# Expert numbers found in two 16-rank steps over all heads, and one-hot rows for spreading made by other engines

## The chip, the core and the metric

The kernel runs on one core of one Trainium2 chip. A core has five engines that run side by side: TensorE (PE in the profile, its weight loads PEld) multiplies matrices, VectorE (DVE), ScalarE (ACT) and GpSimd (POOL) work element by element, and SyncE (SP) starts transfers. Each engine takes its instructions in the order in which they stand in its own queue; semaphores tie the queues together. The metric is the device time of one execution in microseconds (us), lower is better.

## What is computed

One layer of a flow-matching backbone is applied to two streams, a prompt of 256 tokens (P) and a sample of 1024 tokens (Q). After a token mixer comes a layer of 16384 single-neuron experts with product keys. The change lies in that layer alone:

```python
q = (xb @ w_query).reshape(PEER_TOKEN_BLOCK, PEER_HEADS, 2, PEER_HALF)
s = jnp.einsum("thpk,pnk->thpn", q, sub_keys).astype(jnp.float32)
top_s, top_i = lax.top_k(s, PEER_TOPK)
cand_s = top_s[:, :, 0, :, None] + top_s[:, :, 1, None, :]
cand_i = top_i[:, :, 0, :, None] * N_KEYS + top_i[:, :, 1, None, :]
...
best_s, best_j = lax.top_k(cand_s, PEER_TOPK)
idx = jnp.take_along_axis(cand_i, best_j, axis=-1)
g = jax.nn.softmax(best_s, axis=-1)
u = u_tab[idx]
act = jax.nn.gelu(jnp.einsum("td,thkd->thk", xb, u).astype(jnp.float32))
v = v_tab[idx]
return jnp.einsum("thk,thkd->td", (g * act).astype(xb.dtype), v)
```

There are 8 heads, 128 keys on each side, 16 best of each side, and 16 best of their pairs. A token thus has 128 expert numbers (first key times 128 plus second key) and 128 gates.

## The kernel before

Tokens are handled in blocks of 128, one token a partition: two blocks of P, eight of Q. `route` (line 906) chooses the experts of a block. It finds the 16 best of each side by VectorE's eight-at-a-time maximum (lines 917 to 921), adds scores and expert numbers for the 50 pairs that can be among the best 16 (lines 925 to 933, tiles `cs` and `ci`), and finds the 16 best pairs of each head, `bv`, with their places `pu` among the 50 (lines 938 to 942). Then, head by head, it turns places into expert numbers: VectorE compares the 16 places with 50 numbers (`hot`, line 948, 800 elements), GpSimd multiplies by the expert numbers (`oh`, line 950), VectorE sums over the 50 (line 951). Last come the gates `g`, by ScalarE's exponential.

Two ways lead on from there. Blocks of P and the last three of Q go to `experts`: GpSimd gathers the rows of both expert tables one expert at a time for all 128 tokens (tile `row`, line 1010), and VectorE multiplies and adds them (lines 1023 and 1032). These rows run as a long background of the whole kernel. `PACE` ties the gathers of Q to marks that `spread` sets, three gathers to a mark. The first five blocks of Q (`DB`) are computed densely instead: TensorE multiplies all experts, and the gates have to stand in a table of 128 x 128 experts for every token. `spread` (line 1038) makes that table. For four tokens a step, 32 steps a block, it makes one-hot rows of the first key times the gate (`oa`) and of the second key (`ob`), multiplies them on TensorE (line 1068), and ScalarE copies the product into the block's table `G` (line 1069). When 32 steps are done, SyncE stores `G` to memory in eight transfers (line 1071, tile `d_GD`). `G` has one buffer, in the pool `stage`, so the next block fills it only after that store has read it. The one-hots come from one VectorE compare of both keys in bfloat16 (`hot`, line 1058); ScalarE widens the second key's to `ob` (line 1059), and the first key's are multiplied by the gate on GpSimd in one step (line 1061) and on ScalarE, four times a step, in the next (line 1065).

The stage that does this (lines 1257 to 1267) handles the blocks in the order 0, 1, 5, 2, 3, 4, 6, 7, routes each, spreads those below five, and beside that computes the dense first layer of 56 of 128 table tiles (`first_layer`, TensorE's products `bank<-hTh,uh` and the like, with `ul` split off on GpSimd). After it, `dense` does the rest. The order of the instructions on each engine is made by a scheduler that plays the program through when it is built; the code's order is only its starting point, so one edit can move instructions elsewhere.

## Time and profile before

| what | value |
|---|---|
| time, median of 3 runs | 5130.33 us (5128.91 to 5131.31) |
| the profiled execution | 5135.52 us, span 5133.7 us |
| TensorE busy | 4395.7 us, 86% |
| VectorE busy | 4081.8 us, 80% |
| GpSimd busy | 3155.0 us, 61% |
| ScalarE busy | 2023.5 us, 39% |
| TensorE's granted clock, mean | 0.925 of full speed |

The profiled execution is one run of the program with every instruction recorded; its span goes from the first to the last recorded instruction. A busy share over the whole span mixes stages with different limits, so the rows further down are cut to the stretch of 2640 to 3616 us in which blocks are routed and spread. In a row of groups stand the line of the code, engine, operation, output tile <- input tiles, shapes, count, then busy time in us and mean of one in ns, then the idle time of the engine just before and what ended it. In a row of one line or tile stand the shortest, the median and the longest duration in ns, and when the first and the last one started.

### The profile page before, as it was taken

The page shows a single profiled execution, that of the slowest core. Times are in us where ns is not written, and L with a number is a line of the kernel's source. Part 1 is how long each engine was busy: PE and PEld are TensorE (multiplying, and loading weights), DVE is VectorE, ACT ScalarE, POOL GpSimd, SP SyncE. Part 2 cuts the span into 40 slices and gives each one's busy share as a digit, 9 for nine tenths or more (in the row PEclk, how much of TensorE's full clock was granted, in tenths as well). Part 3 has the DMA queues.
Part 4 walks back from the last instruction along what each step waited for, and adds up shares of the span by engine and source line. Part 5 has one row for each costly group of instructions (what it writes and reads, how often), then busy time and mean ns, then how long its engine had stood idle before and what let it go on. Part 6 is the DMA issues. An engine that isn't in the chain of part 4 may idle for free.

```text
span 5133.7 us, 68153 instructions
## 1 busy us (share of the span) xinstructions
PE 4395.7 (86%) x23707; PEld 3804.8 (74%) x23707; DVE 4081.8 (80%) x6816; ACT 2023.5 (39%) x3126; POOL 3155.0 (61%) x2290
## 2 busy tenths in 40 slices
PE   6888788899999779799698887874688999999998
PEld 4676677677777678677587877773566799989997
DVE  7778564999995886566769998895688899888997
ACT  4546333336663112212434766776222222222222
POOL 1456451578886765468665576774556677667764
PEclk8999899999999889899899998995899999999999
DMA  6676646698988953478684478877988999899994
GB/s 212 218 242 196 199 144 234 214 322 293 313 305 320 312 174 99 167 290 327 231 289 153 135 238 267 290 264 245 342 314 322 333 337 340 303 343 337 337 339 155
DMA packets 608774, 1346.80 MB, mean 262 GB/s; under 512 B 63743, under 2 KB 283592, under 8 KB 607917
## 3 DMA queue, kind: packets, MB, share of 16 engines
q0 software_dynamic: 187776, 680.61, 37.7%
q1 hardware_dynamic: 412588, 648.20, 37.6%
q10 hardware_dynamic: 8064, 13.64, 0.7%
q8 instruction: 186, 3.05, 0.2%
q14 instruction: 160, 1.30, 0.1%
HBM read 1177.56 MB, written 164.68 MB: 261 GB/s over the span
## 4 chain that ended last, share of the span: by engine, by line
PE 25%; DVE 15%; DMA 6%; issue 5%; POOL 4%; ACT 3%; SPq 2%; ACTq 0%; POOLq 0%; DVEq 0%
PE bank L150 21%; PE bank L159 3%; DVE row L1023 2%; DVE hot L1058 2%; SPq L1071 2%; POOL row L1010 2%; DVE fi L951 1%; DVE y L1032 1%; DMA row<-in_peer_u,idxQ 1%; ACT G L1069 1%; DMA row<-in_peer_v,idxP 1%; POOL vl L193 1%; ACT oa L1065 1%; ACT ob L1059 1%; DVE gt L1118 1%
## 5 line engine op out<-in xcount | busy, mean ns | idle before, releaser
L1032 DVE SCALAR_TENSOR_TENSOR y<-row,act,y 128x1024 f32<-128x1024 f32 x635 | 814.5, 1283 | 146.4 <-DMA row<-in_peer_v,idxP 111.2
L1023 DVE SCALAR_TENSOR_TENSOR row<-row,h 128x1024 f32<-128x1024 f32 x640 | 762.0, 1210 | 129.2 <-DMA row<-in_peer_u,idxP 60.8
L150 PE MATMUL bank<-hTh,ul 128*128 128x320 f32 x2048 | 641.2, 315 | 16.8 <-POOL ul L193 16.7
L150 PE MATMUL bank<-hTh,uh 128*128 128x320 f32 x2048 | 643.2, 314 | 3.7 <-ACT sc L883 3.6
L150 PE MATMUL bank<-hTl,uh 128*128 128x320 f32 x2048 | 641.9, 314 | 0.0
L150 PE MATMUL bank<-vl,wh 128*128 128x512 f32 x1280 | 513.1, 401 | 50.8 <-POOL vl L193 47.4
L1010 POOL DMA_INDIRECT row<-in_peer_v,idxQ x384 | 409.8, 1067 | 230.9 <-DVE y L1032 176.3
L1010 POOL DMA_INDIRECT row<-in_peer_u,idxQ x384 | 404.9, 1054 | 230.2 <-DVE row L1023 136.3
L150 PE MATMUL bank<-vh,wh 128*128 128x512 f32 x1280 | 473.8, 397 | 76.5 <-ACT vh L192 68.5
L193 POOL TENSOR_TENSOR wl<-wr,wh 128x1024 fp32r<-128x1024 f32 x148 | 362.6, 2451 | 273.7 <-ACT wh L192 252.8
L150 PE MATMUL bank<-vh,wl 128*128 128x512 f32 x1280 | 509.3, 398 | 5.1 <-DVE wl L193 4.9
L150 PEld LDWEIGHTS bank<-hTh,ul 128*128 128x128 f32 x2048 | 390.6, 191 | 20.6 <-POOL ul L193 20.4
L150 PEld LDWEIGHTS bank<-hTh,uh 128*128 128x128 f32 x2048 | 392.0, 191 | 5.7 <-ACT sc L883 3.9
L150 PEld LDWEIGHTS bank<-hTl,uh 128*128 128x128 f32 x2048 | 392.0, 191 | 1.4
L192 ACT ACTIVATE wh<-wr 128x1024 fp32r<-128x1024 f32 x176 | 185.7, 1057 | 463.7 <-PE bank L150 187.6
L1068 PE MATMUL bank<-ob,oa 128*128 128x128 f32 x1280 | 225.6, 327 | 152.2 <-ACT G L1069 74.8
L1010 POOL DMA_INDIRECT row<-in_peer_u,idxP x256 | 272.8, 1065 | 132.3 <-DVE row L1023 73.8
L150 PEld LDWEIGHTS bank<-vh,wh 128*128 128x128 f32 x1280 | 243.8, 191 | 132.7 <-ACT vh L192 72.8
L1010 POOL DMA_INDIRECT row<-in_peer_v,idxP x256 | 277.4, 1083 | 93.7 <-issue 30.6
L150 PEld LDWEIGHTS bank<-vl,wh 128*128 128x128 f32 x1280 | 246.9, 193 | 114.1 <-POOL vl L193 56.5
L1068 PEld LDWEIGHTS bank<-ob,oa 128*128 128x128 f32 x1280 | 196.0, 226 | 179.4 <-ACT G L1069 74.7
L150 PEld LDWEIGHTS bank<-vh,wl 128*128 128x128 f32 x1280 | 246.8, 193 | 59.8 <-DVE wl L193 8.0
(442 smaller groups left out, 12457.6 us busy)
## 6 DMA issues: line engine op xcount, KB each, us to landing
raw<-in_peer_uT SPq DMA_DIRECT2D x128, 512.0 KB
raw<-in_peer_v SPq DMA_DIRECT2D x128, 512.0 KB
wr<-in_w_in SPq DMA_DIRECT2D x112, 512.0 KB
d_GD<-G SPq DMA_DIRECT2D x40, 1024.0 KB
gt<-d_GD SPq DMA_DIRECT2D x128, 320.0 KB
w<-in_w_ada SPq DMA_DIRECT2D x48, 512.0 KB
wr<-in_w_query SPq DMA_DIRECT2D x48, 512.0 KB
d_AD<-a SPq DMA_DIRECT2D x56, 320.0 KB
```

Source lines behind the costliest of these rows:

```text
L150: nc.tensor.matmul(out, l, r, start=(i == 0), stop=(i == len(ops) - 1))
L159: nc.tensor.matmul(out, a, b, start=(i + j == 0), stop=(i == KT - 1 and j == len(ops) - 1))
L192: nc.scalar.activation(hi, src, AF.Copy)
L193: note(eng, eng.tensor_tensor(lo, src, hi.bitcast(F32), op=ALU.subtract))
L951: nc.vector.tensor_reduce(idf[:, h, :], oh[:].rearrange("p c k -> p k c"), axis=AX.X, op=ALU.add)
L1010: i = nc.gpsimd.indirect_dma_start(out=t[:], out_offset=None, in_=A[tab], in_offset=bass.IndirectOffsetOnAxis(ap=idx[:, k:k + 1], axis=0))
L1023: nc.vector.scalar_tensor_tensor(t[:], t[:], 1.0, h[:], op0=ALU.mult, op1=ALU.mult, accum_out=act[:, k:k + 1])
L1032: nc.vector.scalar_tensor_tensor(y[:], t[:], act[:, k:k + 1], y[:], op0=ALU.mult, op1=ALU.add)
L1058: nc.vector.tensor_tensor(hot[:].rearrange("p k t q -> p k (t q)"), keys8[:], key[:, None, t0:t0 + 4, :].rearrange("p o t q -> p o (t q)") ...
L1059: nc.scalar.activation(ob[:], hot[:, :, :, 1].rearrange("p k t -> p t k"), AF.Copy)
L1068: nc.tensor.matmul(ps[:, i * P:(i + 1) * P], oa[:, i, :], ob[:, i, :], start=True, stop=True)
L1071: nc.sync.dma_start(GD[j:j + 16, :, b * P:(b + 1) * P].rearrange("j i t -> i j t"), G[:, j:j + 16, :])
```

## The change

Route: the expert number is no longer summed over 50 places. The pairs stand in rows by the rank of the first key, so a place tells the rank: `FIRSTS` lists at which of the 50 places each rank of 16 begins. For all eight heads at once, 16 chosen slots against 16 ranks (2048 elements in bfloat16), VectorE asks which ranks begin at or before the place, sums the differences of the first keys over those ranks (the sum is the first key itself), takes the largest such beginning and subtracts it (the remainder is the second key's rank), compares that with the 16 ranks and sums the second keys. Each sum or maximum over 16 ranks is a fold by halves: 1024, 512, 256 and 128 elements. GpSimd has no part in it. The two keys stay apart in `ij`; blocks that are spread use them so, and shifting and masking in `spread` goes.

Spread: `ob` is now made by VectorE directly, one compare of float32 numbers with four tokens' second keys (512 elements). `oa` is made by GpSimd in every step, one instruction a token that compares 128 numbers with the token's first key and multiplies by its gate. ScalarE makes neither. `oa` and `ob` have three buffers each instead of two.

```diff
 NCAND = 50
+FIRSTS = [sum(n for _, n in PAIRS[:a]) for a in range(9)] + [43 + a for a in range(7)]
 NEG = -3.0e38
...
-    def numbers(pool, n, w):
-        t = pool.tile([P, n, w], BF, name=f"numbers{n}")
-        nc.vector.tensor_copy(t[:], iota_k[:, 0:n, None].to_broadcast([P, n, w]))
-        return t
+    NS = NH * TOPK
+    def rank_tables(pool):
+        ranks = pool.tile([P, TOPK, NH], BF, name="ranks")
+        nc.vector.tensor_copy(ranks[:], iota_k[:, 0:TOPK, None].to_broadcast([P, TOPK, NH]))
+        firsts = pool.tile([P, TOPK, NH], BF, name="firsts")
+        for a in range(TOPK):
+            nc.vector.memset(firsts[:, a, :], float(FIRSTS[a]))
+        return ranks, firsts
...
             nc.vector.max_index(iu[:, g, 8:16], v[:, g, 8:16], S2[:])
-        fi = peer.tile([P, NH, 2, TOPK], F32, tag="fi", name="fi")
-        nc.vector.tensor_copy(fi[:].rearrange("p h q k -> p (h q) k"), iu[:])
-        nc.vector.tensor_scalar(fi[:, :, 0, :], fi[:, :, 0, :], float(NK), None, op0=ALU.mult)
+        keys = peer.tile([P, 2, TOPK, NH], BF, tag="keys", name="keys")
+        nc.vector.tensor_copy(keys[:], iu[:].rearrange("p (h q) a -> p q a h", q=2))
+        steps = peer.tile([P, TOPK, NH], BF, tag="steps", name="steps")
+        nc.vector.tensor_copy(steps[:, 0, :], keys[:, 0, 0, :])
+        nc.vector.tensor_tensor(steps[:, 1:, :], keys[:, 0, 1:, :], keys[:, 0, 0:TOPK - 1, :], op=ALU.subtract)
         vv = v[:].rearrange("p (h q) k -> p h q k", q=2)
         cs = peer.tile([P, NH, NCAND], F32, tag="cs", name="cs")
-        ci = peer.tile([P, NH, NCAND], F32, tag="ci", name="ci")
-        for dst, src in ((cs, vv), (ci, fi[:])):
-            o = 0
-            for a, n in PAIRS:
-                nc.vector.tensor_tensor(dst[:, :, o:o + n], src[:, :, 1, 0:n], src[:, :, 0, a:a + 1].to_broadcast([P, NH, n]), op=ALU.add)
-                o += n
-            nc.vector.tensor_tensor(dst[:, :, o:o + 8], src[:, :, 0, 8:16], src[:, :, 1, 0:1].to_broadcast([P, NH, 8]), op=ALU.add)
+        o = 0
+        for a, n in PAIRS:
+            nc.vector.tensor_tensor(cs[:, :, o:o + n], vv[:, :, 1, 0:n], vv[:, :, 0, a:a + 1].to_broadcast([P, NH, n]), op=ALU.add)
+            o += n
+        nc.vector.tensor_tensor(cs[:, :, o:o + 8], vv[:, :, 0, 8:16], vv[:, :, 1, 0:1].to_broadcast([P, NH, 8]), op=ALU.add)
         bv = peer.tile([P, NH, TOPK], F32, tag="bv", name="bv")
...
             nc.vector.max_index(pu[:, h, 8:16], bv[:, h, 8:16], c2[:])
-        pf = peer.tile([P, NH, TOPK], BF, tag="pf", name="pf")
-        nc.vector.tensor_copy(pf[:], pu[:])
-        idf = fi[:, :, 0, :]
-        for h in range(NH):
-            hot = peer.tile([P, NCAND, TOPK], BF, tag="hot", name="hot", bufs=1)
-            nc.vector.tensor_tensor(hot[:], places[:], pf[:, h, None, :].to_broadcast([P, NCAND, TOPK]), op=ALU.is_equal)
-            oh = peer.tile([P, NCAND, TOPK], F32, tag="oh", name="oh", bufs=1 if s is SQ else 2)
-            nc.gpsimd.tensor_tensor(oh[:], hot[:], ci[:, h, :, None].to_broadcast([P, NCAND, TOPK]), op=ALU.mult)
-            nc.vector.tensor_reduce(idf[:, h, :], oh[:].rearrange("p c k -> p k c"), axis=AX.X, op=ALU.add)
+        place = peer.tile([P, TOPK, NH], BF, tag="place", name="place")
+        nc.vector.tensor_copy(place[:], pu[:].rearrange("p h k -> p k h"))
+        wide = [P, TOPK, TOPK, NH]
+        flat = lambda t: t[:].rearrange("p a k h -> p a (k h)")
+        mask = peer.tile(wide, BF, tag="mask", name="mask")
+        terms = peer.tile(wide, BF, tag="terms", name="terms")
+        half = peer.tile([P, TOPK // 2, NS], BF, tag="half", name="half")
+        def folded(x, op, dst):
+            x, y, n = flat(x), half[:], TOPK // 2
+            while n:
+                nc.vector.tensor_tensor(dst if n == 1 else y[:, 0:n, :], x[:, 0:2 * n:2, :], x[:, 1:2 * n:2, :], op=op)
+                x, y, n = y, x, n // 2
+        def combine(out, of_rank, of_slot, op):
+            nc.vector.tensor_tensor(out[:], of_rank[:, :, None, :].to_broadcast(wide), of_slot, op=op)
+        slots = lambda t: t[:, None].to_broadcast(wide)
         dense = s is SQ and b < DB
...
         tail = "" if dense else f"{s.name}{b}"
-        idx = keep.tile([P, NH * TOPK], I32, name="idx" + tail)
-        nc.vector.tensor_copy(idx[:].rearrange("p (h k) -> p h k", h=NH), idf)
-        g = keep.tile([P, NH, TOPK], F32, name="gw" + tail)
-        nc.vector.tensor_tensor(g[:], bv[:], bv[:, :, 0:1].to_broadcast([P, NH, TOPK]), op=ALU.subtract)
-        nc.scalar.activation(g[:], g[:], AF.Exp)
+        ij = peer.tile([P, 2, 1, NS], F32, tag="ij", name="ij")
+        base = peer.tile([P, TOPK, NH], BF, tag="base", name="base")
+        combine(mask, firsts, slots(place[:]), ALU.is_le)
+        combine(terms, steps, mask[:], ALU.mult)
+        folded(terms, ALU.add, ij[:, 0])
+        combine(mask, firsts, mask[:], ALU.mult)
+        folded(mask, ALU.max, base[:].rearrange("p (o k) h -> p o (k h)", o=1))
+        nc.vector.tensor_tensor(base[:], place[:], base[:], op=ALU.subtract)
+        combine(terms, ranks, slots(base[:]), ALU.is_equal)
+        combine(terms, keys[:, 1], terms[:], ALU.mult)
+        folded(terms, ALU.add, ij[:, 1])
+        if dense:
+            where = ij[:, :, 0, :]
+        else:
+            where = keep.tile([P, NS], I32, name="idx" + tail)
+            nc.vector.scalar_tensor_tensor(ij[:, 0, 0, :], ij[:, 0, 0, :], float(NK), ij[:, 1, 0, :], op0=ALU.mult, op1=ALU.add)
+            nc.vector.tensor_copy(where[:], ij[:, 0, 0, :])
+        e = peer.tile([P, NH, TOPK], F32, tag="e", name="e")
+        nc.vector.tensor_tensor(e[:], bv[:], bv[:, :, 0:1].to_broadcast([P, NH, TOPK]), op=ALU.subtract)
+        nc.scalar.activation(e[:], e[:], AF.Exp)
         sm = peer.tile([P, NH, 1], F32, tag="sm", name="sm")
-        nc.vector.tensor_reduce(sm[:, :, 0], g[:], axis=AX.X, op=ALU.add)
+        nc.vector.tensor_reduce(sm[:, :, 0], e[:], axis=AX.X, op=ALU.add)
         nc.vector.reciprocal(sm[:], sm[:])
-        nc.vector.tensor_tensor(g[:], g[:], sm[:].to_broadcast([P, NH, TOPK]), op=ALU.mult)
-        return idx, g
-    def routes(s, blocks, rp, places):
+        g = keep.tile([P, TOPK, NH], F32, name="gw" + tail)
+        nc.vector.tensor_tensor(g[:].rearrange("p k h -> p h k"), e[:], sm[:].to_broadcast([P, NH, TOPK]), op=ALU.mult)
+        return where, g[:].rearrange("p k h -> p (k h)")
+    def routes(s, blocks, rp, tables):
         for b in blocks:
-            s.route[b] = route(s, b, rp, places)
+            s.route[b] = route(s, b, rp, *tables)
...
-    def spread(s, b, gp, stage, keys8, GD):
-        idx, g = s.route[b]
-        ii = gp.tile([P, 2, NH * TOPK], I32, tag="ii", name="ii")
-        nc.vector.tensor_scalar(ii[:, 0, :], idx[:], 7, None, op0=ALU.logical_shift_right)
-        nc.vector.tensor_scalar(ii[:, 1, :], idx[:], NK - 1, None, op0=ALU.bitwise_and)
-        ff = gp.tile([P, 2, NH * TOPK], F32, tag="ff", name="ff")
-        nc.vector.tensor_copy(ff[:], ii[:])
+    def spread(s, b, gp, stage, GD):
+        ij, g = s.route[b]
         ps = bank(s)
-        for q, x in enumerate((ff[:, 0, :], ff[:, 1, :], g[:].rearrange("p h k -> p (h k)"))):
+        for q, x in enumerate((ij[:, 0, :], ij[:, 1, :], g)):
             nc.tensor.transpose(ps[:, q * P:(q + 1) * P], x, ident[:])
-        key = gp.tile([P, P, 2], BF, tag="key", name="key", bufs=2)
-        nc.scalar.activation(key[:].rearrange("p t q -> p q t"), ps[:, :2 * P].rearrange("p (q t) -> p q t", q=2), AF.Copy)
-        tr = gp.tile([P, P], F32, tag="tr", name="tr", bufs=2)
-        nc.scalar.activation(tr[:], ps[:, 2 * P:3 * P], AF.Copy)
+        tr = gp.tile([P, 3, P], F32, tag="tr", name="tr", bufs=2)
+        nc.scalar.activation(tr[:].rearrange("p q t -> p (q t)"), ps[:, :3 * P], AF.Copy)
         G = stage.tile([P, NK, P], F32, tag="G", name="G")
         for t0 in range(0, P, 4):
-            oa = gp.tile([P, 4, NK], F32, tag="oa", name="oa", bufs=2)
-            ob = gp.tile([P, 4, NK], F32, tag="ob", name="ob", bufs=2)
-            hot = gp.tile([P, NK, 4, 2], BF, tag="hot", name="hot", bufs=2)
-            nc.vector.tensor_tensor(hot[:].rearrange("p k t q -> p k (t q)"), keys8[:], key[:, None, t0:t0 + 4, :].rearrange("p o t q -> p o (t q)").to_broadcast([P, NK, 8]), op=ALU.is_equal)
-            nc.scalar.activation(ob[:], hot[:, :, :, 1].rearrange("p k t -> p t k"), AF.Copy)
+            oa = gp.tile([P, 4, NK], F32, tag="oa", name="oa", bufs=3)
+            ob = gp.tile([P, 4, NK], F32, tag="ob", name="ob", bufs=3)
+            nc.vector.tensor_tensor(ob[:], iota_k[:, None, :].to_broadcast([P, 4, NK]), tr[:, 1, t0:t0 + 4, None].to_broadcast([P, 4, NK]), op=ALU.is_equal)
+            for i in range(4):
+                t = t0 + i
+                note(nc.gpsimd, nc.gpsimd.tensor_scalar(oa[:, i, :], iota_k[:], tr[:, 0, t:t + 1], tr[:, 2, t:t + 1], op0=ALU.is_equal, op1=ALU.mult))
             if t0 % 8:
-                note(nc.gpsimd, nc.gpsimd.tensor_tensor(oa[:], hot[:, :, :, 0].rearrange("p k t -> p t k"), tr[:, t0:t0 + 4, None].to_broadcast([P, 4, NK]), op=ALU.mult))
                 mark("spread")
-            else:
-                for i in range(4):
-                    nc.scalar.activation(oa[:, i, :], hot[:, :, i, 0], AF.Copy, scale=tr[:, t0 + i:t0 + i + 1])
             ps = bank(s)
...
         SQ.banks = [pa]
-        places, keys8 = numbers(rq, NCAND, TOPK), numbers(sp, NK, 8)
+        tables = rank_tables(rq)
         for b in ORDER:
-            routes(SQ, [b], rq, places)
+            routes(SQ, [b], rq, tables)
             if b < DB:
-                spread(SQ, b, sp, stage, keys8, GD)
+                spread(SQ, b, sp, stage, GD)
         SQ.banks = [pb, pc]
```

The scheduler's order is moved by this. VectorE, in the choice of experts late in the stage, before the change (names: `pf` the places, `oh` GpSimd's products, `row,act` a gathered row's product); in this piece it alternates with a step's compare `hot<-numbers,key`:

```order
L951 TENSOR_REDUCE fi<-oh 128x16
L1058 TENSOR_TENSOR hot<-numbers_22010,key 128x1024
L948 TENSOR_TENSOR hot<-numbers_22008,pf 128x800
L1023 SCALAR_TENSOR_TENSOR row,act<-row,h 128x1024
L1058 TENSOR_TENSOR hot<-numbers_22010,key 128x1024
L1023 SCALAR_TENSOR_TENSOR row,act<-row,h 128x1024 x2
L1058 TENSOR_TENSOR hot<-numbers_22010,key 128x1024
L951 TENSOR_REDUCE fi<-oh 128x16
L948 TENSOR_TENSOR hot<-numbers_22008,pf 128x800
```

The same work after the change, of a block in the same stage (`mask`, `terms`, `half` the wide operations and folds, `ij` the two keys):

```order
L961 TENSOR_TENSOR ij<-half 128x128
L965 TENSOR_TENSOR terms<-steps,mask 128x2048
L926 MAX v<-S_25620 128x8
L926 MAX v<-S_25626 128x8
L946 MATCH_REPLACE c_25544<-bv,cs 128x50
L946 MATCH_REPLACE c_25550<-bv,cs 128x50
L1053 SCALAR_TENSOR_TENSOR row,act<-row,h 128x1024
L961 TENSOR_TENSOR half<-terms 128x1024
L965 TENSOR_TENSOR mask<-firsts,mask 128x2048
L927 MAX_INDEX iu<-v,S_25620 128x8
L927 MAX_INDEX iu<-v,S_25626 128x8
```

The eight pairs of compare and sum by head, each with GpSimd's product between them, have become whole-block operations that wait for no other engine. Counted over the queue, between the first step and the last step of the fourth spread block stood 54 sums by head (8 a block) and 137 gathered rows, and now stand 87 wide operations (17 a block) and 120 gathered rows.

TensorE, where the first layer of the 56 tiles ends, before (`bank<-hTh,ul` the first layer, `bank<-ob,oa` four tokens of spreading, `bank<-ident` the fifth block's transposed keys and gates):

```order
L150 MATMUL bank_29455<-hTl,uh 128x320
L150 MATMUL bank_29455<-hTh,ul 128x320
L1068 MATMUL bank_24937<-ob,oa 128x128 x4
L1068 MATMUL bank_24952<-ob,oa 128x128 x4
L1068 MATMUL bank_24964<-ob,oa 128x128 x4
L1048 MATMUL bank_25213<-ident,ff 128x128 x2
L1048 MATMUL bank_25213<-ident,gw 128x128
L1068 MATMUL bank_25231<-ob,oa 128x128 x4
```

and after:

```order
L156 MATMUL bank_29144<-hTh,ul 128x320
L156 MATMUL bank_29144<-hTh,uh 128x320
L1088 MATMUL bank_24631<-ob,oa 128x128
L156 MATMUL bank_29144<-hTl,uh 128x320
L156 MATMUL bank_29144<-hTh,ul 128x320
L1088 MATMUL bank_24631<-ob,oa 128x128 x2
L1088 MATMUL bank_24644<-ob,oa 128x128 x4
L1088 MATMUL bank_24657<-ob,oa 128x128 x4
```

The first layer now ends at step 117 of the 160, before at step 125, and single tokens' products stand among first-layer products where whole steps stood.

GpSimd, in the steps of the fifth spread block, before (`row<-in_peer_v` a gather):

```order
L1061 TENSOR_TENSOR oa<-hot,tr 128x512
L1010 DMA row<-in_peer_v,idxQ_23601 128x1024 x3
L1061 TENSOR_TENSOR oa<-hot,tr 128x512
L1010 DMA row<-in_peer_v,idxQ_23601 128x1024 x3
L1061 TENSOR_TENSOR oa<-hot,tr 128x512
L1010 DMA row<-in_peer_v,idxQ_23601 128x1024 x2
```

and after:

```order
L1083 TENSOR_SCALAR oa<-iota_k,tr 128x128 x4
L1040 DMA row<-in_peer_v,idxQ_23481 128x1024
L1083 TENSOR_SCALAR oa<-iota_k,tr 128x128 x4
L1040 DMA row<-in_peer_v,idxQ_23481 128x1024 x2
L1083 TENSOR_SCALAR oa<-iota_k,tr 128x128 x4
L1040 DMA row<-in_peer_v,idxQ_23481 128x1024 x2
L1083 TENSOR_SCALAR oa<-iota_k,tr 128x128 x4
L1040 DMA row<-in_peer_v,idxQ_23481 128x1024
```

Two steps have eight instructions where they had one, with three gathers beside them in both. In the fifth block's 32 steps stand 47 gathers, before 36; at the last step 688 gathers are done, before 689.

## Rows read from the trace of the kernel before

**Rows 1.** Busy time by stretch: PE, PEld, DVE, ACT, POOL, then clock, DMA share, GB/s.

```profile
2640.00:2788.00 148.00, 131.10 (x657) 112.91 (x655) 137.96 (x532) 42.31 (x63) 83.01 (x55) 0.94 0.67 218
2788.00:3446.00 658.00, 549.51 (x3584) 526.33 (x3584) 607.90 (x1695) 466.74 (x698) 450.10 (x314) 0.92 0.70 227
3446.00:3485.00 39.00, 3.77 (x16) 3.31 (x16) 13.33 (x14) 8.26 (x15) 9.31 (x9) 0.54 1.04 331
3485.00:3565.00 80.00, 56.01 (x240) 48.37 (x240) 54.33 (x56) 78.05 (x116) 53.52 (x44) 0.63 0.61 184
3565.00:3616.00 51.00, 0.00 (x0) 0.00 (x0) 13.98 (x12) 1.75 (x3) 10.30 (x11) 0.50 1.04 346
3616.00:5133.00 1517.00, 1418.11 (x7296) 1240.86 (x7296) 1317.31 (x1518) 371.02 (x508) 993.01 (x752) 0.98 0.88 317
```

**Rows 2.** The tile G by tile, then its first writes and TensorE's restart from the timeline.

```profile
L1069 ACT ACTIVATE G<-bank x160: 1020/1097/1267, 2795.0 to 3564.2; 128x512 f32<-128x512 f32 x160
...
2961.66 1.92 ACT L1069 ACTIVATE G<-bank 128x512 f32<-128x512 f32 x2 [15.55 <-DMA S<-d_SDQ]
3154.32 1.89 ACT L1069 ACTIVATE G<-bank 128x512 f32<-128x512 f32 x2 [22.40 <-DMA d_GD<-G]
3315.23 1.93 ACT L1069 ACTIVATE G<-bank 128x512 f32<-128x512 f32 x2 [6.62 <-DMA d_GD<-G]
3485.28 1.89 ACT L1069 ACTIVATE G<-bank 128x512 f32<-128x512 f32 x2 [30.39 <-DMA d_GD<-G]
3616.35 2.93 PE L150 MATMUL bank<-vh,wh 128*128 128x512 f32 x6 [52.16 <-ACT vh L192]
```

**Rows 3.** Groups of VectorE instructions, 2788 to 3446 us.

```profile
L1058 DVE TENSOR_TENSOR hot<-numbers,key 128x1024 bf16<-128x1024 bf16 x128 | 153.1, 1206 | 15.6 <-ACT oa L1065 14.9 <-ACT ob L1059 0.6
L951 DVE TENSOR_REDUCE fi<-oh 128x16 f32<-128x800 f32 x54 | 82.7, 1531 | 12.0 <-POOL oh L950 12.0
L948 DVE TENSOR_TENSOR hot<-numbers,pf 128x800 bf16<-128x800 bf16 x53 | 39.0, 736 | 0.0
L931 DVE TENSOR_TENSOR ci<-fi 128x16 f32<-128x16 f32 (+5 forms) x48 | 12.8, 331 | 0.0
```

**Rows 4.** Who TensorE waited for, 2788 to 3446 us: total, times, longest.

```profile
PE bank L1068 <- ACT G L1069: 41.4, 4, 16.9
PE bank L1068 <- ACT oa L1065: 38.0, 22, 5.4
PE bank L1068 <- POOL oa L1061: 11.7, 8, 3.5
```

**Rows 5.** Single VectorE lines: shortest, median, longest duration in ns.

```profile
L1058 DVE TENSOR_TENSOR hot<-numbers,key x160: 658/684/6121, 2787.9 to 3557.7; 128x1024 bf16<-128x1024 bf16 x160
L948 DVE TENSOR_TENSOR hot<-numbers,pf x80: 548/565/2765, 912.2 to 3427.9; 128x800 bf16<-128x800 bf16 x80
L523 DVE TENSOR_TENSOR x<-x,pos x16: 665/686/693, 855.9 to 907.5; 128x512 f32<-128x512 f32 x16
```

**Rows 6.** GpSimd: one line, one group, then the groups of 2788 to 3446 us.

```profile
L796 POOL TENSOR_TENSOR g<-g,y x24: 726/1288/1310, 627.8 to 2384.7; 128x512 f32<-128x512 f32 x16, 128x256 f32<-128x256 f32 x8
masks.py:199 POOL TENSOR_SCALAR_AFFINE_SELECT ident<-ident 128x128 f32<-128x128 f32 x1 | 0.3, 282 | 0.0
...
L950 POOL TENSOR_TENSOR oh<-hot,ci 128x800 f32<-128x800 bf16 x54 | 89.3, 1654 | 93.2 <-DVE hot L948 69.9 <-DVE ci L933 14.5 <-PE bank L150 3.7
L1061 POOL TENSOR_TENSOR oa<-hot,tr 128x512 f32<-128x512 bf16 x64 | 88.9, 1389 | 33.0 <-DVE hot L1058 25.6 <-PE bank L1068 5.2 <-PE bank L150 1.4
```

**Rows 7.** Chain by line, then GpSimd and VectorE groups, 3485 to 3565 us.

```profile
by line: ACT G L1069 36.0%; ACT ob L1059 30.8%; ACT oa L1065 28.8%; DMA d_GD<-G 12.5%; PE bank L1068 4.0%; issue 0.4%; ACTq L1069 0.0%
...
L1010 POOL DMA_INDIRECT row<-in_peer_v,idxQ x30 | 35.5, 1184 | 14.9 <-DVE y L1032 12.5 <-issue 0.8 <-DVE hot L1058 0.3
L1032 DVE SCALAR_TENSOR_TENSOR y<-row,act,y 128x1024 f32<-128x1024 f32 x30 | 38.5, 1283 | 0.1
L1058 DVE TENSOR_TENSOR hot<-numbers,key 128x1024 bf16<-128x1024 bf16 x26 | 18.0, 692 | 49.6 <-ACT oa L1065 49.5
```

More of the change, by code (lines that the diff above doesn't have):

```diff
@@ L903, in new_T, with route @@
         return (pool.tile([P, KT, nb * P], F32R, name="hTh"), pool.tile([P, KT, nb * P], F32R, name="hTl"))
-    def route(s, b, peer, places):
+    def route(s, b, peer, ranks, firsts):
         rows = slice(b * P, (b + 1) * P)
@@ L1002, in experts @@
     def experts(s, blocks, out, peer, ready=None):
-        NS = NH * TOPK
         for b in blocks:
@@ L1024, in experts @@
             nc.scalar.activation(act[:], act[:], AF.Gelu_apprx_tanh)
-            nc.vector.tensor_tensor(act[:], act[:], g[:].rearrange("p h k -> p (h k)"), op=ALU.mult)
+            nc.vector.tensor_tensor(act[:], act[:], g, op=ALU.mult)
             y = pg.tile([P, D], F32, tag="sum", name="y")
@@ L1203, in body @@
                 with tpool(SP, "rt") as rp:
-                    routes(SP, [n // 5], rp, numbers(rp, NCAND, TOPK))
+                    routes(SP, [n // 5], rp, rank_tables(rp))
             if n in SCANS:
```

## Prediction

> **What bounds the kernel now.** I read the busy times by stretch first, then what each engine waits for in the stretch that the change touches, then single durations. The change touches two things: the choice of experts (route) for ten blocks of tokens, and the spreading of five blocks' gates over the table of experts (spread). Nearly all of it lies between 2640 and 3616 us. From 2788 to 3446 us, where the first four spread blocks run, VectorE is busy 607.9 of 658 us (92%), TensorE 549.5, ScalarE 466.7, GpSimd 450.1 [rows 1]. The reader is to see that VectorE is the fullest engine there, and that TensorE, which computes the first layer of 56 table tiles meanwhile, is not far behind. TensorE's own waits in that stretch name ScalarE's one-hots (38.0 us), GpSimd's (11.7) and, with 41.4 us, ScalarE's G, which is stopped by something else: the block's G has one buffer, and the next block may not write it before its store to memory has read it [rows 4].
>
> The ladder of G shows the rhythm. The blocks begin to fill G at 2795.0, 2961.7, 3154.3, 3315.2 and 3485.3 us, and the last write starts at 3564.2 [rows 2]: 167, 193, 161 and 170 us a block, of which about 39 are the store (3446 to 3485, in which TensorE is busy 3.8 us [rows 1]). The fifth block is alone: TensorE has finished the first layer. It takes 80 us for 32 steps, 2.5 us a step, and there the chain is ScalarE for 96% (G 36.0, ob 30.8, oa 28.8) [rows 7]. Then the last store: TensorE idles 52.2 us until the next stage starts at 3616.4 [rows 2]. From there to the end TensorE is busy 1418 of 1517 us [rows 1], with work that the change leaves as it is.
>
> **Route.** Before, each block compares 800 places by head on VectorE, multiplies them on GpSimd and sums them on VectorE. In the four-block stretch that is 54 sums of 1.531 us (82.7), 53 compares of 0.736 (39.0) and the sums of expert numbers (12.8): 134.5 us for 54/8 = 6.75 blocks, 20 us a block, and 89.3 us on GpSimd [rows 3, 6]. After, a block has five operations on 2048 bfloat16 elements and three folds (1024, 512, 256, 128 elements), all on VectorE. The trace has no operation of 2048 elements. The nearest rows are compares of 800 and 1024 bfloat16 elements, at least 0.548 and 0.658 us: 0.49 ns an element, so 1.16 us for 2048, 0.41 for 512, 0.29 for 256 and 0.22 for 128 [rows 5]. Five times 1.16 is 5.8, three folds of 1.58 are 4.7, the small copies and differences come to some 1.4 (seven at about 0.2): 11.9 us. The bound above is the float32 rate: 512 elements take 0.686 us [rows 5], so 2048 about 2.4 us and a block about 20 us, no gain. Between them lie the waits that a two-input operation meets here: the 1024-element compare has a median of 0.684 us [rows 5] but a mean of 1.206 [rows 3]. With 0.5 us on each of the five large ones I take 14.5 us.
>
> The order of the changed kernel puts 87 of the 17 wide operations per block, 5.1 blocks, between the first step and the last step of the fourth block, where 6.75 stood; 1.65 blocks' worth slips into the fifth block, where VectorE has room. So VectorE there loses 134.5 and gains 5.1 x 14.5 = 74. Ahead of the first step 1.3 blocks are routed in both orders, with VectorE busy 138.0 of 148 us [rows 1]: 1.3 x (20 - 14.5) = 7, and with the hand-over to GpSimd gone I take **9 us** (bounds 0 and 15). The two prompt blocks are routed far earlier, beside the input projection of the other stream, whose products hide them; I count them as nothing. If that cover is not there they are worth 2 x 5.5 = 11 us, for or, by a worse order around them, against.
>
> **Spread, VectorE.** One bfloat16 compare of 1024 elements per step becomes a float32 compare of 512. Undisturbed these cost the same, 0.684 and 0.686 us [rows 5]. The old one is drawn out to 1.206 us on average in the four-block stretch [rows 3], yet to 0.692 in the fifth block [rows 7]. I read the difference as waiting for GpSimd, whose long work stands in the first stretch. The new compare also reads two tensors, so I let it keep the 0.52 us: no gain. If the wait vanished, 128 x 0.52 = 67 us would come off VectorE. The Trainium skill (GPSIMD Engine Reference, Specifications) says that GpSimd shares its memory interfaces with VectorE, in contention with VectorE instructions that have two inputs in SBUF; by that rule the compare keeps its wait, which is the zero above, and without it the saving would be the 67 us. The last-block mean agrees with the rule.
>
> **Spread, ScalarE.** It loses ob in every step and oa in every second one, and keeps G. It was the bound only in the fifth block (96% of the chain) and is late nowhere after: what is late next there is GpSimd.
>
> **Spread, GpSimd.** It now makes every step's oa in four instructions of 128 elements with two per-token numbers. No such instruction is in the trace. From below: the one-input operation of 128 elements, 0.282 us [rows 6]. From above: two-input operations take 0.726 us for 256 and 1.288 for 512 elements [rows 6], 2.2 ns an element, so 0.445 for 128. I take 0.37 us, nearer to neither, since the instruction has one tensor input and two small ones: 1.48 us a step. The Trainium skill (GPSIMD Engine Reference, Engine selection) calls one-input elementwise work roughly line-rate; 128 cycles at the page's 1.2 GHz would be an estimate of 0.11 us, the fifth block would fall to VectorE's 75 us, and the sum would come out 16 us lower. The one row of that kind, 0.282 us, is dearer than the rule. In the four-block stretch GpSimd loses 89.3 (oh) and 88.9 (oa) and gains 128 x 1.48 = 189: level, about 460 us.
>
> **Sum of the four-block stretch.** The order has 17 fewer gathered rows in it (120 for 137), 17 x 1.28 [rows 7] = 22 us. VectorE: 607.9 - 134.5 + 74 - 22 = 525 us; at the old 92%, 568 us of length. TensorE then rules: its 549.5 us, the 41.4 of G that the store keeps, and for the waits on one-hots half of the old 49.7, since GpSimd now makes all of them in order behind its gathers: 549.5 + 41.4 + 25 = 616. That is **42 us** less than 658 (bounds: 0, if all waits stay, and 67, if the one-hots are never late).
>
> **Fifth block.** The order ends the first layer at step 117 of 160 (before: 125), and gives this block 47 gathers on GpSimd where 36 stood. Three steps can be made during the store, since oa and ob have three buffers. The other 29 cost GpSimd 29 x 1.48 = 43 us and, with 43 gathers at 1.1 (the row says 1.184 with queueing [rows 7]), 47 us: 90 to 91 us instead of 80. VectorE needs 29 x 0.69 + 43 x 1.283 = 75 and is covered. So **11 us are lost** (bounds 0 at 0.28 us a token, 24 at 0.46). The stores, 39 and 52 us of standstill, stay. The number of gathers done by the last step is the same (688 for 689), so the last stage inherits no backlog.
>
> Sum: -9 - 42 + 11 = **-40 us**. The profiled execution took 5135.5 us (span 5133.7 and 1.8 around it), 5.2 above the median of 5130.3; set against the median this is 5090 us.
>
> **Rivals.**
> (A) TensorE hardly waits for one-hots, because ScalarE is out of the pairing: 549.5 + 41.4 = 591, -67, and -9 + 11: 5065 us. For it: the order now spreads each step's four products singly among first-layer products. Against: each of them now waits for its own GpSimd instruction.
> (B) The gain in the four-block stretch is given back in full. The order packs about 54.4 first-layer tiles ahead of the fourth block's last step, where 53.1 stood; with all 50 us of one-hot waits kept, the stretch stays 658 us and the total is 5130.3 - 9 + 11, 5132 us. For it: TensorE at 549.5 of 658 is the next engine at once.
> (C) **Slower:** GpSimd becomes the bound, by the price of a token's instruction. Without its old oh, oa and the 17 gathers GpSimd keeps 450.1 - 89.3 - 88.9 - 18 = 254 us in the stretch; at 0.7 us a token 512 of them make 612, some 645 us long at 95%, and the fifth block 29 x 2.8 + 47 = 128: -9 - 13 + 48, with 10 more for the products that wait singly, 5165 us. It decides from about 0.6 us a token. For it: no row shows such an instruction, and each reads two per-token numbers; against it the rows of 0.282 us for 128 and 0.726 for 256 elements [rows 6].
> (D) The wide operations run at the float32 rate: a block of 20 us, VectorE 525 + 28 = 553, 599 us at 92%, still below TensorE's 616, and only the 7 of the start go: 5097 us. It hides inside the forecast.
>
> **How the numbers follow.** Forecast with D 0.45 (5070 to 5112 us), A 0.23, B 0.17, C 0.15. This measurement can tell about 0.2% from no change, 10 us. Faster by more than that (below 5120): forecast, A and a small part of B, 0.70; slower (above 5140): C and what of B goes over, 0.17; within: 0.13. The range of 8 in 10 goes from A with its bounds (start -15, stretch -67, fifth block 0, with some of the 67 us of vanished waits: 5035) to B with a dear token (5145).
>
> **What would show it.** Right: the token instruction at 0.28 to 0.45 us; the 2048-element operations at 1.2 to 1.7 us; the blocks of G some 155 to 165 us apart; the fifth block 85 to 100 us from first to last write of G; ScalarE absent from TensorE's waits but for G. Wrong: GpSimd's token instruction at 0.6 us or more, or TensorE waiting for oa for 50 us and more in the four blocks, or a last stage, from the last store on, that is longer than before by over 10 us.

## The result and the profile after

The changed kernel is slower: 5273.65 us, median of 4 runs (5267.90 to 5281.57), against 5130.82 us (5128.91 to 5135.92) for the kernel before on the same chip. The ratio is 1.0279, 95% interval 1.0264 to 1.0295. The profiled execution has a span of 5265.8 us, 132.1 more than before's 5133.7.

Busy time of the changed kernel by stretch, cut at its own steps (ahead of the first step; first step to last write of the fourth block, as in the second row of [rows 1]; the store behind it; fifth block; last store; last stage); the columns are those of [rows 1]:

```profile
2640.00:2752.00 112.00, 99.95 (x501) 85.41 (x500) 111.21 (x456) 35.38 (x53) 56.05 (x34) 0.95 0.70 228
2752.00:3511.00 759.00, 622.35 (x3653) 575.97 (x3651) 486.13 (x1629) 247.94 (x314) 718.88 (x693) 0.85 0.57 188
3511.00:3547.00 36.00, 6.29 (x16) 4.00 (x16) 29.04 (x53) 0.42 (x2) 31.00 (x28) 0.50 1.09 348
3547.00:3695.00 148.00, 87.75 (x240) 58.22 (x240) 76.60 (x72) 32.34 (x32) 134.38 (x151) 0.51 0.50 153
3695.00:3745.00 50.00, 0.00 (x0) 0.00 (x0) 15.34 (x13) 1.40 (x2) 13.16 (x14) 0.50 1.06 360
3745.00:5265.00 1520.00, 1420.96 (x7296) 1243.59 (x7296) 1321.69 (x1520) 371.68 (x508) 1003.03 (x752) 0.97 0.88 317
```

The last of the five busy times is GpSimd's: 718.9 of 759 us (95%) and 134.4 of 148 (91%), where it had 450.1 of 658 and 53.5 of 80 [rows 1]. VectorE fell to 486.1, below the 525 of the prediction, and nothing gets faster by it: it idles 170 us of the stretch before gathered rows, whose transfers GpSimd issues. The last stage is 1520 us (before 1517).

The lines of GpSimd's token instruction, of VectorE's `ob` and of one of the wide operations (shortest, median, longest in ns), and below them GpSimd's largest group from 2752 to 3511 us, with its mean of 909 ns:

```profile
L1083 POOL TENSOR_SCALAR oa<-iota_k,tr x640: 783/790/2959, 2749.9 to 3693.0; 128x128 f32<-128x128 f32 x160
L1080 DVE TENSOR_TENSOR ob<-iota_k,tr x160: 665/692/3576, 2752.3 to 3680.2; 128x512 f32<-128x512 f32 x160
L965 DVE TENSOR_TENSOR terms<-steps,mask x10: 1210/1221/1237, 915.7 to 3525.2; 128x2048 bf16<-128x2048 bf16 x10
```

```profile
L1083 POOL TENSOR_SCALAR oa<-iota_k,tr 128x128 f32<-128x128 f32 x512 | 461.3, 909 | 8.2 <-PE bank L1088 6.2
```

The token instruction never took less than 0.783 us; the prediction had 0.37, with 0.445 as its upper bound. Its mean is 0.909 in the four blocks, so 512 of them are 461.3 us, and a step costs GpSimd 3.6 us instead of 1.48.

Who TensorE waited for in the same stretch (total in us, times, longest):

```profile
PE bank L1088 <- POOL oa L1083: 63.0, 87, 3.0
PE bank L156 <- POOL ul L199: 50.2, 28, 6.4
PE bank L156 <- ACT uh L198: 10.7, 11, 2.9
PE bank L1088 <- ACT G L1089: 9.5, 3, 4.5
```

Two of these rows are GpSimd's. `oa` itself is late, and so is `ul`, the half of the first layer's weights that GpSimd splits off: it stands in the same queue. ScalarE's G, the largest wait before [rows 4], is down to 9.5 us. That is not because the next block's one-hots come too late: the last product ahead of a block's first write of G is done 17 to 23 us before that write (2923.1 for 2939.7, 3524.4 for 3546.9). Why TensorE's wait for G shrank is not shown.

The ladder of G has its first writes at 2758.1, 2939.7, 3148.3, 3349.4 and 3546.9 us and the last at 3694.6. Against [rows 2] the 132 us fall into four parts: start -36.9, four blocks +98.5 (788.8 for 690.3), fifth block +68.8 (147.7 for 78.9), last stage with its store +1.6.

### The profile page after: what moved, and what is told of

Read it like the earlier page. It is cut to its first block, busy times and chain, and to the rows that moved or that the text cites. A ratio compares the mean times of both kernels' runs of the same rounds, so it can differ in the third digit from the quotient of the medians.

```text
span 5265.8 us, 68030 instructions
## 1 busy us (share of the span) xinstructions
PE 4488.7 (85%) x23707; PEld 3855.2 (73%) x23707; DVE 3976.7 (76%) x6788; ACT 1744.5 (33%) x2638; POOL 3494.8 (66%) x2770
## 4 chain that ended last, share of the span: by engine, by line
PE 25%; POOL 10%; DVE 9%; issue 7%; DMA 7%; SPq 2%; ACT 1%; POOLq 0%; DVEq 0%; ACTq 0%
PE bank L156 22%; POOL oa L1083 4%; POOL row L1040 3%; PE bank L165 2%; SPq L1091 2%; DMA row<-in_peer_v,idxQ 2%; DVE y L1062 2%; POOL ul L199 1%; DMA row<-in_peer_u,idxQ 1%; DVE row L1053 1%; PE bank L1088 1%; DVE gt L1138 1%; DMA gt<-d_GD 1%; DMA row<-in_peer_v,idxP 1%; POOL wl L199 1%
## 5 line engine op out<-in xcount | busy, mean ns | idle before, releaser
L156 PE MATMUL bank<-hTh,ul 128*128 128x320 f32 x2048 | 653.4, 324 | 50.2 <-POOL ul L199 50.2
L156 PE MATMUL bank<-hTh,uh 128*128 128x320 f32 x2048 | 662.8, 324 | 10.9 <-ACT uh L198 10.7
L156 PE MATMUL bank<-hTl,uh 128*128 128x320 f32 x2048 | 656.0, 320 | 0.0
L1083 POOL TENSOR_SCALAR oa<-iota_k,tr 128x128 f32<-128x128 f32 x640 | 574.8, 906 | 15.9 <-PE bank L1088 12.7
L1088 PE MATMUL bank<-ob,oa 128*128 128x128 f32 x1280 | 320.4, 355 | 165.2 <-POOL oa L1083 130.2
L156 PEld LDWEIGHTS bank<-hTh,uh 128*128 128x128 f32 x2048 | 403.3, 197 | 15.4 <-ACT uh L198 13.5
L1088 PEld LDWEIGHTS bank<-ob,oa 128*128 128x128 f32 x1280 | 239.7, 233 | 232.4 <-POOL oa L1083 197.1
L156 PEld LDWEIGHTS bank<-vh,wh 128*128 128x128 f32 x1280 | 244.1, 191 | 128.3 <-ACT vh L198 68.8
```

Source lines behind the costliest of these rows:

```text
L156: nc.tensor.matmul(out, l, r, start=(i == 0), stop=(i == len(ops) - 1))
L1083: note(nc.gpsimd, nc.gpsimd.tensor_scalar(oa[:, i, :], iota_k[:], tr[:, 0, t:t + 1], tr[:, 2, t:t + 1], op0=ALU.is_equal, op1=ALU.mult))
L1088: nc.tensor.matmul(ps[:, i * P:(i + 1) * P], oa[:, i, :], ob[:, i, :], start=True, stop=True)
```

## The experiments

Nine kernels ran: the eight from `route_only` on in the table, and a program that prices single instructions. Times are medians; ratios are to the kernel before on the same chip, with 95% intervals. The last two columns are from one profiled execution each: the last write of G, behind which only the last store and the last stage are left.

| kernel | us | ratio | last write of G | from there to the end |
|---|---|---|---|---|
| before | 5131 | 1 | 3564.2 | 1569.5 |
| changed | 5273.7 | 1.0279 (1.0264 to 1.0295) | 3694.6 | 1571.1 |
| route_only | 5033.1 | 0.9813 (0.9797 to 0.9830) | 3466.5 | 1570.4 |
| spread_only | 5366.3 | 1.0474 (1.0454 to 1.0494) | 3789.5 | 1568.7 |
| half_vector | 5075.8 | 0.9894 (0.9872 to 0.9917) | 3471.8 | 1610.5 |
| cheap_token | 5090.2 | 0.9925 (0.9902 to 0.9948) | 3502.4 | 1574.4 |
| pool_mult | 5094.3 | 0.9922 (0.9903 to 0.9941) | 3528.0 | 1576.2 |
| all_vector | 5100.6 | 0.9937 (0.9913 to 0.9961) | 3438.8 | 1657.3 |
| fifth_copy | 5032.2 | 0.9801 (0.9783 to 0.9819) | 3462.6 | 1568.3 |
| route_dummy | 5102.0 | 0.9940 (0.9919 to 0.9961) | 3538.1 | 1563.5 |

The theories at the start: P, the price of GpSimd's token instruction makes the change slow; O, the order does (single products, each behind an instruction of its own); R, the new route does. Within P stood whether the price is fixed, or per element, or comes from the pointers to per-token numbers, or from VectorE beside it.

### The two halves alone

`route_only` is the changed kernel with the old `spread`; `spread_only` is the kernel before with the new one.

> The changed kernel's choice of experts with the old one-hots of spread. Theory P: 5040 to 5095 us, since the choice of experts saves 17 us ahead of the stage and 30 to 60 in it, and the whole loss lies in GpSimd's per-token instructions. Rival R (the new choice of experts, or the order that the scheduler makes of it, is a loss of its own): 5130 us or more.

> The old choice of experts with the new one-hots of spread. Theory P: 5260 to 5340 us, GpSimd busy over 90% of the four-block stretch, with oh on top of the 640 per-token instructions. Rival R: 5110 to 5150 us.

The new route alone gains 92 us (5125.2 before on that chip), the new spread alone loses 241. Their sum, +149, is what the whole change costs (+143). R falls, and the loss is all in the new spread. Both expectations were too timid: each half is larger than its range.

### The price, by itself

A program of its own, no part of the model, that runs each form four times on GpSimd, then twelve token instructions while VectorE makes 512-element compares. It computes nothing of the layer. Its lines, shortened:

```diff
+for i in range(4): gpsimd.tensor_scalar(pp, iota[:, 0:128], s[:, 2*i], s[:, 2*i+1], op0=is_equal, op1=mult)
+    ... pp of 512; ii: constants; p: is_equal alone; e: mult alone; m: add, mult; tt: tensor times tensor
+for i in range(12): gpsimd.tensor_scalar(both, ..., op0=is_equal, op1=mult)   # beside:
+for i in range(20): vector.tensor_tensor(with_v, iota[:, 0:512], s broadcast, op=is_equal)
```

> Not the computation: single GpSimd and VectorE instructions on an idle core, four of each form, then twelve per-token instructions beside a stream of VectorE compares; the outputs are left at zero. Theory P (price): the per-token instruction (128 elements, compare and multiply with two per-partition numbers) costs 0.75 to 0.8 us on GpSimd with nothing beside it, and not much more beside VectorE. Theory W (waiting): alone it costs 0.28 to 0.45 us, and the 0.79 to 0.91 us of the changed kernel come from VectorE's two-input compares beside it. What the price is made of: if fixed per instruction, 512 elements cost about 1.0 to 1.3 us; if per element, 2.8 us or more; if it is the two per-partition numbers, the form with constants is at 0.3 to 0.4 us.

Single lines of that program: shortest, median and longest duration in ns.

```profile
L41 POOL TENSOR_SCALAR pp<-iota,s x4: 791/792/794, 2.5 to 4.9; 128x128 f32<-128x128 f32 x4
L45 POOL TENSOR_SCALAR pp<-iota,s x4: 2065/2066/2117, 12.6 to 18.8; 128x512 f32<-128x512 f32 x4
L47 POOL TENSOR_SCALAR ii<-iota x4: 635/637/718, 20.9 to 22.8; 128x128 f32<-128x128 f32 x4
L51 POOL TENSOR_SCALAR p<-iota,s x4: 597/597/777, 31.2 to 33.2; 128x128 f32<-128x128 f32 x4
L53 POOL TENSOR_SCALAR e<-iota,s x4: 599/602/792, 33.7 to 35.7; 128x128 f32<-128x128 f32 x4
L55 POOL TENSOR_SCALAR m<-iota,s x4: 441/445/448, 36.3 to 37.5; 128x128 f32<-128x128 f32 x4
L59 POOL TENSOR_TENSOR tt<-iota x4: 455/455/456, 41.0 to 42.3; 128x128 f32<-128x128 f32 x4
L61 POOL TENSOR_TENSOR tt<-iota,s x4: 1041/1042/1042, 42.7 to 45.7; 128x512 f32<-128x512 f32 x4
L68 DVE TENSOR_SCALAR dpp<-iota,s x4: 334/382/719, 9.2 to 13.4; 128x128 f32<-128x128 f32 x4
L76 POOL TENSOR_SCALAR both<-both,s x12: 787/1396/1752, 46.7 to 61.7; 128x128 f32<-128x128 f32 x12
L79 DVE TENSOR_TENSOR with_v<-iota,s x20: 700/766/6085, 41.2 to 59.6; 128x512 f32<-128x512 f32 x20
```

Alone, a token instruction takes 0.79 us, the floor that the kernel shows. From 128 to 512 elements it grows by 1.27 us: 3.3 ns an element and some 0.37 us fixed, between the two that were expected; one wide instruction would still cost 2.07 us a step. The pointers are worth 0.15 us (0.79 with them, 0.64 with constants) when it compares and multiplies; but adding and multiplying with the same two pointers takes 0.445 us, as little as the product of two tensors (0.455). So it is the operation: compare-and-multiply is dear on this engine, add-and-multiply is not. A compare alone and a product with one number alone both take 0.60, so the dear thing isn't the compare as such; what makes add-and-multiply cheap was not looked into. VectorE does the same instruction in 0.334 us at its shortest.

The last two rows are the load from the neighbour. Beside back-to-back VectorE compares the token instruction takes 1.396 us (0.787 when they had ended), where "not much more" than alone was expected; VectorE's compare has a median of 0.766 and a shortest of 0.700. The Trainium skill (GPSIMD Engine Reference, Specifications) says that the two engines contend for their memory interfaces when VectorE has two inputs in SBUF; these rows agree, and here GpSimd pays far more than VectorE. Beside GpSimd's products of two tensors it is the other way round: the longest compare, 6.085 us, began at 41.18 us with GpSimd's eight products (`tt`, 41.05 to 46.72) and ended at 47.27, while the products took their 0.455 and 1.04 us.

The traces of the kernels show both. In the changed kernel 222 token instructions ran with no two-tensor instruction of VectorE beside them and took 0.792 us on average, the other 418 took 0.967. So the neighbour costs some 0.11 us on average (0.906 for 0.792), and the rest is the price of the form. In the kernel before, 90 of the 160 compares `hot` ran with no product or split of two tensors on GpSimd beside them and took 0.681 us on average, at most 0.725; the other 70 took 1.650 on average (0.66 to 6.12).

### The price, in the kernel

`cheap_token` changes one word, so that the dear form becomes the cheap one.

```diff
-... tr[:, 0, t:t + 1], tr[:, 2, t:t + 1], op0=ALU.is_equal, op1=ALU.mult)
+... tr[:, 0, t:t + 1], tr[:, 2, t:t + 1], op0=ALU.add, op1=ALU.mult)
```

> The changed kernel with one word altered: GpSimd's token instruction adds the key and multiplies by the gate, where it compared and multiplied. The rows are then no one-hots and G is wrong; count, place, operands and sizes stay, and few instructions change places. Alone, this form took 0.445 us where compare-and-multiply took 0.79. Theory P (the price of the compare on GpSimd): the token instruction at 0.44 to 0.55 us, GpSimd some 254 + 512 x 0.5 = 510 us in four blocks, TensorE waits for it 40 us or less, time 5030 to 5120. Theory O (many small instructions on GpSimd and single products in order behind them): no price helps, time above 5200.

Its token instruction, and its stretches (first write of G to fifth block, fifth block):

```profile
L1083 POOL TENSOR_SCALAR oa<-iota_k,tr x640: 437/442/2583, 2750.8 to 3501.1; 128x128 f32<-128x128 f32 x160
```

```profile
2756.00:3390.00 634.00, 521.60 (x3419) 502.87 (x3419) 524.70 (x1655) 237.45 (x296) 545.04 (x703) 0.91 0.70 230
3390.00:3503.00 113.00, 86.27 (x480) 78.08 (x480) 75.78 (x72) 42.15 (x50) 101.30 (x148) 0.76 0.62 196
```

The median of 0.442 us is the upper bound of the prediction (the mean from 2756 to 3390 us is 0.574), and the time is 5090.2 us: 44 below before on that chip, and by the ratios 182 below the changed kernel. The same instructions, at a price of 0.44 instead of 0.79, take back most of the loss. That the time is the forecast's 5090 is luck: against before the start gave 38.6 us and not 9, the four blocks 56.5 and not 42, the fifth block lost 33.4 and not 11, and the end lost 4.9. Theory O falls as the main cause: a single token's product stands alone among other products 279 times here, 258 times in the changed kernel and 15 times before, and this doesn't make it slow. The order isn't held to the last row: the scheduler moved instructions with this operation, and to turn the one queue into the other at least 14% of GpSimd's 2770 instructions and 18% of VectorE's would have to change places. By the ratios 57 us remain to `route_only`.

### Where else the token instructions could go

`half_vector` gives every second step's four token instructions to VectorE, `all_vector` all of them.

```diff
-                note(nc.gpsimd, nc.gpsimd.tensor_scalar(oa[:, i, :], ...))
+                eng = nc.gpsimd if t0 % 8 else nc.vector     # half_vector
+                note(eng, eng.tensor_scalar(oa[:, i, :], ...))
```

> The changed kernel, but every second step's four per-token instructions on VectorE. Theory P: GpSimd's 3.6 us a step are halved, 254 + 256 x 0.91 = 487 us in the four-block stretch, VectorE 515 + 64 x 4 x 0.2 = 570; TensorE sets 600 to 640 us; the fifth block 16 x 3.6 + 47 = 105 us: 5040 to 5110 us in all. Theory O (the loss lies in the order of the queues, single tokens' products among first-layer products, whatever a token costs): stays above 5200 us. Theory W: VectorE's instructions are drawn out instead, 5150 to 5250 us.

> The changed kernel with all token instructions on VectorE, none on GpSimd. VectorE's own work in the spread stretch is 586 us in the changed kernel; 640 instructions at 0.33 to 0.44 us add 210 to 280: some 800 to 870 us, so VectorE becomes the bound and the time is 5150 to 5260, worse than the halves (5076). Rival: VectorE's instructions are drawn out mainly by GpSimd's work beside them; with that gone they run at 0.33 and 0.69 us and the time is below 5076.

`half_vector` came out as expected; `all_vector` between its two theories, since both were partly right. Its stretches (four blocks, fifth block, from the last write of G to the end), and then what GpSimd waited for from 2766 to 3439 us:

```profile
2766.00:3349.00 583.00, 489.50 (x3366) 475.08 (x3365) 578.73 (x1857) 228.53 (x284) 213.13 (x141) 0.95 0.66 217
3349.00:3439.00 90.00, 76.82 (x528) 74.24 (x528) 88.57 (x252) 47.43 (x57) 29.82 (x20) 0.94 0.48 156
3439.00:5096.00 1657.00, 1421.53 (x7296) 1241.78 (x7296) 1456.84 (x1805) 372.29 (x511) 1081.76 (x835) 0.93 0.90 323
```

```profile
POOL row L1040 <- DVE row L1053: 188.5, 39, 21.9
POOL ul L199 <- ACT uh L198: 139.7, 22, 19.0
```

VectorE is full (578.7 of 583 us), and yet spreading ends earliest of all kernels. What VectorE left undone are the gathered rows: GpSimd's gathers wait 188.5 us for VectorE to release their buffers, 108 of 768 are done at the last write of G (186 in `route_only`), and from there to the end, where VectorE is busy 1456.8 us and in the changed kernel 1337.0, it takes 88 us longer than before. `half_vector` has the same debt in small: 131 gathers done, 41 us longer. So VectorE's time is not free either: here it is paid for later.

### Every step on GpSimd, at the old price

`pool_mult`, shown against `route_only`, keeps the new route, the old compare and ScalarE's `ob`, but GpSimd multiplies by the gates in every step, one instruction of 512 elements.

```diff
-            if t0 % 8:
-                note(nc.gpsimd, nc.gpsimd.tensor_tensor(oa[:], hot[...], tr[...], op=ALU.mult))
-                mark("spread")
-            else: ... four nc.scalar.activation(oa[:, i, :], ...)
+            note(nc.gpsimd, nc.gpsimd.tensor_tensor(oa[:], hot[...], tr[...], op=ALU.mult))
+            if t0 % 8:
+                mark("spread")
```

> New route, old compare on VectorE and old ob on ScalarE, but GpSimd multiplies the first key's one-hots by the gates in all steps (one instruction of 512 elements), and ScalarE in none. If the price of a step on GpSimd is what matters (1.33 us here, 3.6 us in the changed kernel), GpSimd is busy 443 + 64 x 1.33 = 530 of 700 us and the time is 5005 to 5060, near that of the new route alone (5033). If it is the assignment of every step to GpSimd, behind its gathers, TensorE waits for it 80 us and more and the time is above 5100.

Neither range held it. TensorE's waits from 2772 to 3528 us, with the largest of `route_only` (2769 to 3467 us) below:

```profile
PE bank L1096 <- POOL oa L1091: 80.7, 58, 3.5
PE bank L1096 <- ACT G L1097: 65.8, 3, 32.1
```

```profile
PE bank L1099 <- ACT G L1100: 58.2, 4, 19.6
PE bank L1099 <- ACT oa L1096: 27.9, 20, 3.1
PE bank L1099 <- ACT ob L1090: 14.4, 22, 1.3
PE bank L1099 <- POOL oa L1092: 8.5, 11, 2.4
```

With 1.36 us a step GpSimd is busy 548 of 756 us, and still TensorE waits 80.7 us for it, where the shared work had 50.8 in all. GpSimd's step itself waited 57.4 us for VectorE's compare; for the rest I suspect the gathers and weight splits ahead of it in the queue, which no run separates. So giving GpSimd every step has a cost of its own, 56 us against `route_only` by the ratios, about what `cheap_token` still lost. It is the smaller part; the price of compare-and-multiply, 182 us, is the larger.

### What the route's gain is made of

`route_dummy` is `route_only`, and GpSimd does eight multiplications a block that nobody reads, as many as the old route had.

```diff
         folded(terms, ALU.add, ij[:, 1])
+        spare = terms[:].rearrange("p a k h -> p (a k h)")
+        for h in range(NH):
+            nc.gpsimd.tensor_tensor(spare[:, 0:800], spare[:, 800:1600], spare[:, 1200:2000], op=ALU.mult)
```

> New route, old one-hots, and behind the choice of each block GpSimd does eight multiplications of 800 bfloat16 elements that nobody reads, as many as it lost with the old route (89 us in the four-block stretch). New route alone took 5033 us. Theory V (the route's gain is VectorE's time): 5028 to 5045. Theory G (part of the gain is that GpSimd no longer stands in the way of the first layer's weight split and of the one-hots): 5055 to 5100, and TensorE waits again for the weight split, as before (16.7 us) or longer.

The dummies in the spread stretch, and who TensorE waited for there (2769 to 3530 us):

```profile
L989 POOL TENSOR_TENSOR terms<-terms 128x800 bf16<-128x800 bf16 x59 | 102.4, 1736 | 28.3 <-DVE half L967 26.1
```

```profile
PE bank L1102 <- ACT oa L1099: 38.5, 26, 5.7
PE bank L1102 <- POOL oa L1095: 25.5, 17, 4.8
PE bank L162 <- POOL ul L205: 6.7, 6, 2.0
```

5102 us: by the ratios (0.9940 and 0.9813) 65 of the 96 us that the route gains are gone. The first write of G comes 23 us later than in `route_only`, the four blocks take 645 instead of 607 us, the fifth 100 instead of 90. Two thirds of the route's gain thus go when GpSimd has eight products a block again, and the theory that all is VectorE's own time falls. The expected sign did not show: TensorE waits 6.7 us for the weight split, less than the 16.7 before, and the one-hots are what is late (38.5 and 25.5 us for 27.9 and 8.5). Nor do the dummies act by GpSimd's queue alone: VectorE is busy 554 us in the four blocks with them and 535 without, its additions to `cs` taking 0.53 us on average for 0.27. The dummies also wait for VectorE's folds (26.1 us), so they may hold the queue a little more than the old instructions did.

### The fifth block

`fifth_copy` is `route_only`, and in the fifth block VectorE copies `ob` out of the compare in every second step.

```diff
+            if b == 4 and t0 % 8 == 0:
+                nc.vector.tensor_copy(ob[:], hot[:, :, :, 1].rearrange("p k t -> p t k"))
+            else:
                 nc.scalar.activation(ob[:], hot[:, :, :, 1].rearrange("p k t -> p t k"), AF.Copy)
```

> New route alone, and in the fifth spread block VectorE copies ob out of the compare in every second step, where ScalarE did. If ScalarE bounds that block (G 1.1, ob 1.1 and on average half of 2.1 us for oa in a step), 16 copies of 1.1 us leave it: the block takes 75 to 82 us instead of 90, and the time is 5015 to 5030. If GpSimd's gathers and steps bound it, nothing changes: 5028 to 5040.

The block takes 83.9 us instead of 90.0, just outside the 75 to 82 expected, and the time (0.9801) can't be told from `route_only` (0.9813), as the rival had it. If the 6 us, read from one execution each, are real, ScalarE is a part of that block's pace, a smaller one than expected. These two kernels beat both that were given.

## Why the prediction was wrong, step by step

- **GpSimd's token instruction, the step that failed.** The prediction put 0.37 us between 0.282 and 0.445; it took 0.906 on average, 0.79 with nothing beside it. The lower row was an instruction with another operation, the upper bound a two-input product. None of the rows used was a compare on GpSimd, and the bounds were taken from the element rate of other operations as if the operation didn't matter. 0.445 is right for a product or for add-and-multiply (`cheap_token` 0.442) and wrong for compare-and-multiply. No price beside a busy VectorE was put on it, either (0.967 for 0.792).
- **The four-block stretch, -42.** It came to +98.5. GpSimd "level, about 460 us" was 718.9. The TensorE rule under it (549.5 + 41.4 + 25) would have needed one-hots that come in time.
- **The fifth block, +11.** It came to +68.8. At the block's own mean of 0.840 us a token, 29 steps and 43 gathers at 1.03 (44.5 us) are 142; measured 147.7. The formula was nearly right, its price wrong. (Its upper bound, 24 us at 0.46, comes out at 20.)
- **Rival C** had mechanism, place and formula: 254 us and the 461.3 of the tokens are 715, 753 at its 95%; the stretch took 759 (to its last write, as its 645 was meant), and GpSimd was busy 718.9. It had a chance of 0.15, and its own price of 0.7 was too low. (By its own sums it decides from 0.65 us a token, not 0.6.) The trace of before showed no instruction of the kind, so its upper side should have stayed open, and the range with it.
- **Start, -9.** It came to -36.9 (`route_only` -25.7). Of the latter 23 us are gone again with `route_dummy`'s products; I had some 2 us for that hand-over.
- **Route on VectorE.** The 2048-element operations had medians of 1.22 to 1.23 us, and means of 1.22 to 1.66 in the stretch, for 1.16 + 0.5. VectorE's 525 us were 486.1, of which `ob` explains 33 (120.5 us for 153.1). Rival D is out. What I missed is that the freed `oh` is on the path: I entered its 89.3 us only in GpSimd's own sum. In `route_only` TensorE no longer waits for `ul` at all (16.7 us before), and the four blocks take 607 us instead of 690.
- **`ob` keeps half of its wait.** Median 0.692 us, mean 0.952 in the four blocks, for 1.2: between the two bounds. It was read rightly as waiting for GpSimd, but the wait comes with GpSimd's instructions on two tensors, and the new `oa` is none: 138 of the 160 compares with no product or split of two tensors beside them took 0.725 us on average, 22 with one 2.114.
- **The last stage** was right: 1520 for 1517 us. My sign of a wrong prediction, TensorE waiting 50 us and more for `oa`, is the first row of its waits: 63.0.
- **Not in the sum: TensorE's own time.** For nearly the same work (3818, 3895 and 3863 recorded products) it was busy 604.5 us in before's five blocks at a mean granted clock of 0.87, 712.8 in the changed kernel's at 0.78, and 584.3 in `route_only`'s at 0.92. In the fifth block of the changed kernel, where TensorE is busy 87.8 of 148 us, the mean is 0.51, about the lower of its two levels (1.2 of 2.4 GHz). I read this as the waits costing more than themselves, so that what removes them gives more back; no run sets the clock by itself.

## What to carry to other kernels

Price an instruction by its engine and its operation: with no row of that operation on that engine, a row of another one with as many elements is not an upper bound, and four instructions of it in every step of a loop deserve a measurement first. Work that is taken off an engine counts wherever another engine waits for that queue or is held up beside it, not only in its own sum; and work that is put on a full engine may seem free in its stretch and come due later as a backlog. When a change has two halves, run them apart: here one was worth 92 us and the other cost 241.
